# Router of a mixture of experts: the first pair of experts gathered in float32, the high and low halves split later, filler matmuls on TensorE

## Chip, cores and metric

One core of one Trainium2 chip. The metric is the device time of one launch in microseconds (us); the median of three runs of the kernel before is 2560.29 us. Everything is float32 at the interface; weights come from HBM.

## The reference

Two transformer layers (each a mixer, a layer norm, a hierarchical mixture of experts and a layer norm), and behind them a second block of other layers that the change doesn't touch. What matters here is the mixture of experts, once per layer, on 256 tokens of width 1024:

```python
xf = x.reshape(n, d)                                   # 256 x 1024
grp_logits = xf @ w_grp + b_grp                        # 4 groups
g_idx = argmax(grp_logits); p_grp = softmax(grp_logits)[g_idx]
exp_logits = (xf @ w_exp + b_exp).reshape(n, 4, 8)
top_l, top_e = lax.top_k(exp_logits[g_idx], 2)         # two experts of the group
gate = p_grp[:, None] * softmax(top_l)
...
hdn = silu(xb @ w_gate[e]) * (xb @ w_up[e])            # 1024 -> 512
y = hdn @ w_down[e]                                    # 512 -> 1024
out[token] += gate * y
x = layer_norm(ALPHA * x + out)
```

The 32 experts have 6 MB of weights each, and all of them are read in each layer.

## The kernel before, in words

**Stages.** Mixer of layer 0, mixture of experts 0 ("stage 0"), mixer of layer 1, mixture of experts 1 ("stage 1"), then the second block. An expert gets 64 slots; tokens beyond that go through a loop at the end (line 957 on) that the change doesn't touch.

**Weights.** `load_pair` (line 692) issues twelve loads of 1 MB for two experts: four of gate, four of up, four of down. All are issued on SP's queue, in a fixed order, and each waits there until its buffer is free; what stands behind a waiting load waits too. The buffers form a ring of 18 slots (`moe_ring`: the tags W, V, S, X, H and last `c_phase`). The slots belong to tensors of the mixer or the router until these are dead. The last slot, `c_phase`, holds the gain and bias rows of the first layer norm (`rows`, shown as `phase` in the profile), whose last reader is `residual`. Load 19 uses the first slot again.

**The router** (`moe`, line 680 on). `ln_norm` normalises the tokens: ScalarE takes the first 128, VectorE the second. The logits were already multiplied in `Moe.feed` while the mixer ended; `logits` corrects them for mean and deviation. `first_max` finds the group and the two experts on VectorE, a chain of some twenty small dependent operations that ends in `sel` (`m_sel`). In program order behind it stands `hilo` on the normalised tokens, four times: ScalarE casts a piece to fp32r (`xh`), VectorE subtracts (`xl`). Two matmuls with triangular and all-ones matrices (`lt`) turn `sel` into positions `pos`.

**The first gather.** `hots(0)` compares positions with slot numbers and gives one-hot matrices for four experts (`m_P`), and the same scaled by the gates (`m_PG`). `gather` multiplies `xh` and `xl` with the one-hots, 256 slots at once, and ScalarE evacuates with the norm's gain and bias into `xg`. Then `residual` writes ALPHA times the normalised tokens (with gain and bias rows) over the tokens themselves (`r_out = xn`), in four operations on VectorE. The factor `al` is made from an element of the one-hots, so that the scheduler can't put the residual ahead of them.

**The loop over 16 pairs.** `gate_up` (64 matmul instructions in the trace), `hidden`, `down`, and the scatter of the pair before; every second pair gathers the next four experts. TensorE's order in the loop is the program's; elsewhere the tile scheduler orders each engine.

Of the kernel before, what the change touches and what calls it, by code (L numbers as in the profile page):

```python
# [8 lines left out]
F32 = mybir.dt.float32  # L9
F32R = mybir.dt.float32r  # L10
I32 = mybir.dt.int32
U8 = mybir.dt.uint8
AF = mybir.ActivationFunctionType
ALU = mybir.AluOpType
# [3 lines left out]
P = 128  # L18
D = 1024
T = 256  # L20
ALPHA = 4.0 ** 0.25
# [8 lines left out]
NT4 = 2  # L30
NX = 4
NH = 9


C2 = {}
# [90 lines left out]
class K:  # L126
# [33 lines left out]
    def H(self, dt=F32):  # L160
        return self.big.tile([P, NH_F], dt, name=self.nm("H"), tag="H", bufs=NH)

# [150 lines left out]

    def ln_norm(self, out, r, between=None):

        mu, rs = self.ln_stats(r)
        nb = self.tl([P, 2], "ln_nb", 2)
        self.stt(nb, mu, -1.0, rs, ALU.mult, ALU.mult)
        if between is not None:
            between(nb, rs)  # L320
        self.act(out[:, 0], r[:, 0], AF.Identity, scale=rs[:, 0:1], bias=nb[:, 0:1])
        self.ts(out[:, 1], r[:, 1], rs[:, 1:2], ALU.mult, nb[:, 1:2], ALU.add)
        return nb, rs


# [49 lines left out]


def mixer_a(k, x_tm, moe):

    A, nc = k.A, k.nc
# [219 lines left out]
def bc(ap, shape):  # L599
    return ap.to_broadcast(shape)  # L600


class Moe:
# [49 lines left out]
    def feed(self, r, c):  # L653

        k, V = self.k, self.k.nc.vector
        if self.rT is None:
            self.rT = k.H()[:, :2048].rearrange("p (k t) -> p k t", k=8)
            self.lps = [k.pq(), k.pq()]
        for j in range(2 * c, 2 * c + 2):
            ps = k.pq()  # L660
            for m in range(2):
                kk = 2 * j + m
                for i in range(2):
                    k.tr(ps[:, (2 * m + i) * P : (2 * m + i + 1) * P], r[:, i, kk * P : (kk + 1) * P])
            v = ps.rearrange("p (k t) -> p k t", k=2)
            k.acopy(self.rT[:, 2 * j], v[:, 0])
            V.tensor_copy(self.rT[:, 2 * j + 1], v[:, 1])
        for kk in range(4 * c, 4 * c + 4):
            for i in range(2):
                k.mm(self.lps[i][:, 0:36], self.rT[:, kk, i * P : (i + 1) * P], self.wgb[:, 0, kk, :],  # L670
                     start=kk == 0, stop=kk == 7)
# [6 lines left out]
def moe(k, l, r_in, bufs, gb, rows, csb, lps, lt, then):  # L678
    A, nc = k.A, k.nc
    V = nc.vector  # L680
    wg, wu, wd = A["moe_w_gate"][l], A["moe_w_up"][l], A["moe_w_down"][l]
    cst = k.c_m
    iota1 = cst[:, 128:192]
# [3 lines left out]
    def ld(src, kk, n):  # L687
        w = k.wslot()[:, : kk * n].rearrange("p (k f) -> p k f", k=kk)
        k.dma(w, src)
        return w  # L690

    def load_pair(es):

        out = [([], [], []) for _ in es]
        for n, (w, kk, h) in enumerate([(wg, 8, 0), (wg, 8, 1), (wu, 8, 0), (wu, 8, 1), (wd, 4, 0), (wd, 4, 1)]):
            for j, e in enumerate(es):
                v = w[e].rearrange("(p k) f -> p k f", p=P)[:, h * kk // 2 : (h + 1) * kk // 2, :]
                out[j][n // 2].append(ld(v, kk // 2, v.shape[2]))
        return out

    ws0 = load_pair([0, 1])


    xn, xh, xl = (t[:, :2048].rearrange("p (i d) -> p i d", i=2) for t in bufs)
# [34 lines left out]
    sel = k.tl([P, 2, 32], "m_sel", 1, F32R)  # L739
# [2 lines left out]
    k.add(v48(sel), oh1, oh2)  # L742
    k.mul(v48(sel), v48(sel), og)

    perm = lambda t, i, c: t[:, i].rearrange("t (k p) -> t k p", k=8)[:, :, c // 8 : c // 8 + 64]
    for i in range(2):
        for c in range(0, 1024, 512):
            k.hilo(perm(xh, i, c), perm(xl, i, c), xn[:, i, c : c + 512].rearrange("t (p k) -> t k p", k=8))

    pps = k.pq()  # L750
    for j in range(2):
        k.mm(pps[:, 64 * j : 64 * j + 64], lt[:, j], sel.rearrange("p i e -> p (i e)"))
    pos = k.tl([P, 2, 32], "m_pos", 1)
    cnt = k.tl([P, 32], "m_cnt", 1)
    V.tensor_copy(cnt, pps[:, 64:96])
    k.stt(pos[:, 0], pps[:, 0:32], 1.0, sel[:, 0], ALU.add, ALU.mult)
    k.stt(pos[:, 1], pps[:, 32:64], 1.0, cnt, ALU.add, ALU.add)
    k.mul(pos[:, 1], pos[:, 1], sel[:, 1])
    k.add(cnt, cnt, pps[:, 96:128])

    for j in range(2):
        k.mul(m4[:, 2], m4[:, j], ohg)
# [11 lines left out]
    G = k.tl([P, 2, 32], "m_G", 1)  # L774
# [7 lines left out]
    nb = k.tl([P, 32], "m_nb", 1)  # L782
# [6 lines left out]
    for s in (1, 2, 4, 8, 16):  # L789
        a, b = c0[:, cur], c0[:, 1 - cur]  # L790
# [31 lines left out]

    r_out = xn

    def residual(pt):

        al = k.tl([P, 1], "m_al", 1)
        k.ts(al, pt[:, 1, 255:256], 0.0, ALU.mult, ALPHA, ALU.add)
        for i in range(2):
            k.stt(r_out[:, i], xn[:, i], al, rows[:, 0:1024], ALU.mult, ALU.mult)  # L830
            k.stt(r_out[:, i], rows[:, 1024:2048], al, r_out[:, i], ALU.mult, ALU.add)

    def gather(pt, n, out):

        per = 512 // n
        for j in range(0, 8, per):
            ps = k.pq()
            for m in range(per):
                o = ps[:, m * n : (m + 1) * n]
                f = slice((j + m) * P, (j + m + 1) * P)  # L840
                for i in range(2):
                    k.mm(o, xh[:, i, f], pt[:, i], start=i == 0, stop=False)
                    k.mm(o, xl[:, i, f], pt[:, i], start=False, stop=i == 1)
            for m in range(per):
                kk = j + m
                k.act(out[:, kk], ps[:, m * n : (m + 1) * n], AF.Identity, scale=gb[:, 0, kk : kk + 1], bias=gb[:, 1, kk : kk + 1])

    def gate_up(ws, xg, s0):

        gu = []  # L850
        for m in range(2):
            ps = k.pd()
            for kk in range(8):
                for j in range(2):
                    k.mm(ps[64 * j : 64 * j + 64, :], xg[:, kk, s0 + 64 * j : s0 + 64 * j + 64], ws[j][m][kk // 4][:, kk % 4, :],
                         start=kk == 0, stop=kk == 7)
            gu.append(ps)
        return gu
# [40 lines left out]
    def onehots(pos_v, g_v, n):  # L899

        pt = k.tl([P, 2, n * 64], "m_P", 1, F32R)
        pg = k.tl([P, 2, n * 64], "m_PG", 1)
        v = lambda t: t.rearrange("p i (e s) -> p i e s", e=n)
        for i in range(2):
            sh = [P, n, 64]
            io = bc(iota1[:, None, :], sh)
            k.tt(v(pt)[:, i], io, bc(pos_v[:, i, :, None], sh), ALU.is_equal)
            k.mul(v(pg)[:, i], v(pt)[:, i], bc(g_v[:, i, :, None], sh))
        return pt, pg

    def transposed(pg, o):
        ps = k.pq()
        for i in range(2):
            k.tr(ps[:, i * P : (i + 1) * P], pg[:, i, o : o + P])
        return ps[:, :T]

    def slots(pg, o):

        ps = transposed(pg, o)
        oh, gs = k.tl([P, T], "m_pgT", 2, F32R), k.tl([P, 1], "m_gs", 2)  # L920
        k.red(gs, ps, ALU.add)
        k.ts(oh, ps, 0.0, ALU.is_gt)
        return oh, gs

    def hots(q):
        return onehots(pos[:, :, 4 * q : 4 * q + 4], G[:, :, 4 * q : 4 * q + 4], 4)

    def gathered(pt):
        xg = k.H()[:, :2048].rearrange("p (k s) -> p k s", k=8)
        gather(pt, 256, xg)  # L930
        return xg

    pt, pg = hots(0)
    xg = gathered(pt)
    residual(pt)
    prev = None
    with k.tc.manual_schedule(engines={mybir.EngineType.PE}):
        for p in range(16):
            q, o = p // 2, P * (p % 2)
            ws = load_pair([2 * p, 2 * p + 1]) if p else ws0  # L940
            g, u = gate_up(ws, xg, o)
            oh, gs = slots(pg, o)
            if o and q < 7:
                pt, pg = hots(q + 1)
                xg = gathered(pt)
            hT = hidden(g, u)
            if prev is not None:
                scatter(*prev)
            prev = (oh, *down(ws, hT, gs))
        scatter(*prev)  # L950
# [6 lines left out]
    with k.tc.For_i(0, n_ov, 1) as it:  # L957
# [4 lines left out]
        e = nc.sync.value_load(evi[0:1, ds(it, 1)], min_val=0, max_val=31)  # L962
        ws = ([], [], [])
        for n, (w, kk, h) in enumerate([(wg, 8, 0), (wg, 8, 1), (wu, 8, 0), (wu, 8, 1), (wd, 4, 0), (wd, 4, 1)]):
            v = w[ds(e, 1)][0].rearrange("(p k) f -> p k f", p=P)[:, h * kk // 2 : (h + 1) * kk // 2, :]
            ws[n // 2].append(ld(v, kk // 2, v.shape[2]))
        pt, pg = onehots(pc, gc, 1)
        xg = k.H()[:, :512].rearrange("p (k s) -> p k s", k=8)
# [8 lines left out]
        for m in range(2):  # L977
            ps = k.pd()
            for kk in range(8):
                for j in range(2):  # L980
                    k.mm(half(ps, j)[:, :256], xg[:, kk, :], ws[m][kk // 4][:, kk % 4, 256 * j : 256 * j + 256],
                         start=kk == 0, stop=kk == 7)
            gu.append(ps[:, :256])
        g, u = gu
# [17 lines left out]
        for i in range(2):  # L1002
            for j in range(2):
                ps = k.pq()
                k.mm(ps, half(pgT, j)[:, i * P : (i + 1) * P], half(y, j))
                o = r_out[:, i, j * 512 : (j + 1) * 512]
# [870 lines left out]
def body(tc, A, out):  # L1877
    from contextlib import ExitStack

    with ExitStack() as es:  # L1880
# [3 lines left out]
        with tc.tile_pool(name="b1", bufs=1) as b1:  # L1884
            k.big = b1
            dense_ring = w + [("V", NV, b1, 2048)] * NV
            moe_ring = dense_ring + [("S", 1, b1, 2048)] + [("X", NX, b1, 2048)] * NX + [("H", NH, b1, NH_F)] * 4 + [("c_phase", 1, b1, 2048)]
            k.set_ring(dense_ring)
# [103 lines left out]
```

## Time and profile before

| | |
|---|---|
| runs | 2560.29, 2560.14, 2571.59 us; median 2560.29 |
| profiled execution | 2567.35 us, of which the span is 2565.5 us |
| busy share of the span | TensorE 93%, VectorE 54%, ScalarE 41% |
| mean granted TensorE clock | 0.975 |
| mean DMA rate | 251 GB/s |
| stage 0, first gate matmul | 172.69 us |
| stage 1, first gate matmul | 837.98 us |

Times in the trace count from the start of the span. PE is TensorE's matmul, PEld its weight load, DVE VectorE, ACT ScalarE, SP the engine that issues the DMAs. L184 is the helper for matmuls, L187 for transposes, L190 for activations, L193 for copies on ScalarE, L196 for tensor-tensor operations, L213 for the fused scalar-tensor-tensor operations, L181 for DMAs; so tile names tell more than lines. A row of windows gives start and end, length, busy time and count for each engine, granted clock, DMA share and GB/s.

### The profile page before, as it was taken

How to read it: one execution, taken by the hardware profiler on the slowest of the kernel's cores; microseconds unless marked ns; L12 is line 12 of the kernel's file. 1: busy time of each engine (PE TensorE's matmuls, PEld its weight loads, DVE VectorE, ACT ScalarE, POOL GpSimd, SP SyncE). 2: the span in 40 equal slices, each digit the busy share in tenths (PEclk: the TensorE clock that was granted, in tenths of full speed). 3: DMA queues.
4: the chain of work that ended last, by engine and by line, in shares of the span. 5: the costliest groups of instructions: out<-in, count | busy, mean ns of one | idle time of the engine just before them, and what ended most of it. 6: DMA issues, size and time to landing. Idle time of an engine off the chain costs nothing.

```text
span 2565.5 us, 38758 instructions
## 1 busy us (share of the span) xinstructions
PE 2383.6 (93%) x15416; PEld 1748.8 (68%) x15416; DVE 1379.7 (54%) x2844; ACT 1062.1 (41%) x2138; POOL 18.5 (1%) x27
## 2 busy tenths in 40 slices
PE   8979998988787999889979999999998999999999
PEld 7754433334665443333368988899998898889999
DVE  6962222212676322222268878756556887766654
ACT  3421211111532211111147775646454777565654
POOL 0000000000200000000000000000000000000000
PEclk9989999999888999999979999999999999999999
DMA  8569999998535899999945533355553553445553
GB/s 302 168 267 420 421 420 421 420 421 361 183 131 197 366 420 420 421 420 420 400 155 182 173 108 125 107 168 163 179 179 118 186 169 108 134 130 181 181 181 115
DMA packets 189821, 644.14 MB, mean 251 GB/s; under 512 B 21891, under 2 KB 36277, under 8 KB 139589
## 3 DMA queue, kind: packets, MB, share of 16 engines
q1 hardware_dynamic: 189636, 641.63, 66.6%
q8 instruction: 122, 2.00, 0.3%
q14 instruction: 63, 0.51, 0.1%
HBM read 640.46 MB, written 1.12 MB: 250 GB/s over the span
## 4 chain that ended last, share of the span: by engine, by line
PE 53%; DMA 13%; DVE 5%; ACT 3%; issue 1%; ACTq 0%; SPq 0%; DVEq 0%
PE pd L184 44%; PE pq L184 7%; DMA w<-in_moe_w_up 5%; DMA w<-in_moe_w_down 5%; DMA w<-in_moe_w_gate 3%; PE pq L187 2%; DVE Y L196 1%; ACT Y L193 1%; DVE r L213 0%; ACT cb L190 0%; DVE H L196 0%; ACT r L190 0%; DVE cb L209 0%; DVE Xl L196 0%; DVE sg L209 0%
## 5 line engine op out<-in xcount | busy, mean ns | idle before, releaser
L184 PE MATMUL pd<-U,Y 128*128 128x272 f32 (+1 forms) x7792 | 1011.4, 288 | 18.6 <-ACT U L193 12.8
L184 PEld LDWEIGHTS pd<-U,Y 128*128 128x128 f32 x7792 | 979.8, 189 | 35.2 <-ACT U L193 14.2
L196 DVE TENSOR_TENSOR Y<-w,Y 128x1024 fp32r<-128x1024 f32 x344 | 419.6, 1222 | 265.1 <-ACT Y L193 262.4
L184 PE MATMUL pd<-w,H 128*64 128x512 f32 (+1 forms) x2112 | 483.9, 592 | 53.6 <-DMA w<-in_moe_w_up 37.8
L193 ACT CAST Y<-w 128x1024 fp32r<-128x1024 f32 x344 | 359.4, 1047 | 329.8 <-PE pd L184 299.3
L184 PEld LDWEIGHTS pd<-w,H 128*64 128x64 f32 x2112 | 159.1, 138 | 371.7 <-issue 257.1
L184 PE MATMUL pd<-w,m_hT 128*64 128x512 f32 x1040 | 230.4, 595 | 1.8 <-ACT m_hT L193 1.8
L184 PEld LDWEIGHTS pd<-w,m_hT 128*64 128x64 f32 x1040 | 71.6, 137 | 143.0 <-issue 139.0
L213 DVE SCALAR_TENSOR_TENSOR t4k<-pd,m_gs,t4k 128x512 fp32r<-128x512 f32 x64 | 48.1, 751 | 194.4 <-ACT t4k L190 191.9
L196 DVE TENSOR_TENSOR t2k<-t2k,pd 128x512 f32<-128x512 f32 (+1 forms) x33 | 22.4, 679 | 229.0 <-PE pd L184 229.0
L190 ACT ACTIVATE t4k<-pd,m_gs 128x512 fp32r<-128x512 f32 x64 | 44.0, 687 | 235.8 <-PE pd L184 132.1
L213 DVE SCALAR_TENSOR_TENSOR t2k<-t2k,pd 128x512 f32<-128x512 f32 (+1 forms) x33 | 22.4, 680 | 217.8 <-ACT t2k L190 217.8
L190 ACT ACTIVATE H<-pq,m_gb 128x256 f32<-128x256 f32 (+1 forms) x136 | 62.7, 556 | 147.5 <-PE pq L184 147.5
L190 ACT ACTIVATE t2k<-pd 128x512 f32<-128x512 f32 (+1 forms) x37 | 21.9, 591 | 233.4 <-PE pd L184 233.4
L184 PE MATMUL pd<-Xh,H 128*128 128x512 f32 (+1 forms) x320 | 105.6, 402 | 4.3 <-ACT H L193 4.2
L196 DVE TENSOR_TENSOR H<-H,pq 128x512 f32<-128x512 f32 x132 | 82.0, 682 | 26.3 <-PE pq L184 26.3
L193 ACT COPY m_hT<-pq 128x512 f32<-128x512 f32 (+1 forms) x34 | 19.6, 577 | 175.2 <-PE pq L187 170.3
L213 DVE SCALAR_TENSOR_TENSOR r<-pd,cw,r 128x270 f32<-128x270 f32 (+1 forms) x192 | 87.8, 492 | 3.9 <-ACT r L190 2.4
L193 ACT CAST Xh<-w 128x2048 fp32r<-128x2048 f32 (+4 forms) x34 | 57.3, 1689 | 70.4 <-PE pd L184 54.2
L184 PE MATMUL pd<-Z,Y 128*128 128x272 f32 (+1 forms) x512 | 84.2, 286 | 0.0
L196 DVE TENSOR_TENSOR Xl<-w,Xh 128x2048 fp32r<-128x2048 f32 (+4 forms) x34 | 69.0, 2033 | 27.0 <-ACT Xh L193 26.8
L184 PE MATMUL pd<-H,Xh 128*128 128x256 f32 (+1 forms) x352 | 68.7, 296 | 7.0 <-DVE H L196 4.6
(397 smaller groups left out, 2565.6 us busy)
## 6 DMA issues: line engine op xcount, KB each, us to landing
w<-in_moe_w_gate SPq DMA_DIRECT2D x130, 1024.0 KB
w<-in_moe_w_down SPq DMA_DIRECT2D x130, 1024.0 KB
w<-in_moe_w_up SPq DMA_DIRECT2D x130, 1024.0 KB
w<-in_w_in SPq DMA_DIRECT2D x76, 1024.0 KB
w<-in_w_mlp_up SPq DMA_DIRECT2D x32, 1024.0 KB
w<-in_w_mlp_down SPq DMA_DIRECT2D x32, 1024.0 KB
w<-in_w_ssd_down SPq DMA_DIRECT2D x16, 1024.0 KB
w<-in_ev_w_in SPq DMA_DIRECT2D x14, 1024.0 KB
```

The lines of the kernel that those rows point to most:

```text
L184: return self.nc.tensor.matmul(out, l, r, start=start, stop=stop, **kw)
L187: return self.nc.tensor.transpose(out, in_, self.ident[: in_.shape[0], : in_.shape[0]])
L190: return self.nc.scalar.activation(out, in_, func, **kw)
L193: return self.nc.scalar.copy(out, in_)
L196: return self.nc.vector.tensor_tensor(out=out, in0=a, in1=b, op=op)
L213: return self.nc.vector.scalar_tensor_tensor(out=out, in0=a, scalar=s, in1=b, op0=op0, op1=op1)
```

## The change

1. `ln_norm` in the router: both halves of the tokens are normalised by ScalarE. In `feed` the last two transposed banks are copied by ScalarE alone.
2. Twelve filler matmuls (`FILL`), `ones` times a piece of the tokens ahead of the norm, go to a bank that nobody reads.
3. The positions take four smaller matmuls, which add the second half's offset in PSUM; VectorE then makes `pos` in one operation.
4. The first pair is gathered from the normalised tokens themselves: `xn` in float32 against the one-hots of two experts (`hot0(0)`), evacuated half by ScalarE and half by VectorE into `xgs[:, 0]`.
5. The one-hots of experts 2 and 3 and all four `hilo` are held behind the last two evacuations (`issue_after`). The second pair is gathered the old way, in TensorE's program behind the first pair's gate and up, into `xgs[:, 1]`.
6. `residual` takes the constant ALPHA, without the dependency on the one-hots.

```diff
     def ln_norm(self, out, r, between=None):
         self.act(out[:, 0], r[:, 0], AF.Identity, scale=rs[:, 0:1], bias=nb[:, 0:1])
-        self.ts(out[:, 1], r[:, 1], rs[:, 1:2], ALU.mult, nb[:, 1:2], ALU.add)
+        if between is not None:
+            self.act(out[:, 1], r[:, 1], AF.Identity, scale=rs[:, 1:2], bias=nb[:, 1:2])
+        else:
+            self.ts(out[:, 1], r[:, 1], rs[:, 1:2], ALU.mult, nb[:, 1:2], ALU.add)
...
+            if c:
+                k.acopy(self.rT[:, 2 * j : 2 * j + 2], v)
+            else:
+                k.acopy(self.rT[:, 2 * j], v[:, 0])
+                V.tensor_copy(self.rT[:, 2 * j + 1], v[:, 1])
...
+    idle = k.pd()
+    for j in range(FILL):
+        k.mm(idle[:, 0:256], k.ones, r_in[:, 1, 512:768])
...
     pps = k.pq()
-    for j in range(2):
-        k.mm(pps[:, 64 * j : 64 * j + 64], lt[:, j], sel.rearrange("p i e -> p (i e)"))
+    k.mm(pps[:, 0:64], lt[:, 0], sel.rearrange("p i e -> p (i e)"), start=True, stop=False)
+    k.mm(pps[:, 32:64], lt[:, 1], sel[:, 0], start=False, stop=True)
+    for i in range(2):
+        k.mm(pps[:, 64:96], lt[:, 1], sel[:, i], start=i == 0, stop=i == 1)
...
+    hot0(0)
+    xgs = k.H()[:, :2048].rearrange("p (h k s) -> p h k s", h=2, k=8)
+    for j in range(0, 8, 4):
+        ps = k.pq()
+        for m in range(4):
+            o = ps[:, m * P : (m + 1) * P]
+            for i in range(2):
+                k.mm(o, xn[:, i, j + m :: 8], pt0[:, i, 0:128].bitcast(F32), start=i == 0, stop=i == 1)
+        for m in range(4):
+            kk = j + m
+            o, g, b = ps[:, m * P : (m + 1) * P], gb[:, 0, kk : kk + 1], gb[:, 1, kk : kk + 1]
+            if m % 2:
+                ev_d = k.ts(xgs[:, 0, kk], o, g, ALU.mult, b, ALU.add)
+            else:
+                ev_a = k.act(xgs[:, 0, kk], o, AF.Identity, scale=g, bias=b)
...
+    with k.tc.issue_after(ev_a.ins), k.tc.issue_after(ev_d.ins):
+        hot0(2)
+        for i in range(2):
+            for c in range(0, 1024, 512):
+                k.hilo(perm(xh, i, c), perm(xl, i, c), xn[:, i, c : c + 512].rearrange("t (p k) -> t k p", k=8))
...
-    def residual(pt):
-        al = k.tl([P, 1], "m_al", 1)
-        k.ts(al, pt[:, 1, 255:256], 0.0, ALU.mult, ALPHA, ALU.add)
+    def residual():
         for i in range(2):
-            k.stt(r_out[:, i], xn[:, i], al, rows[:, 0:1024], ALU.mult, ALU.mult)
-            k.stt(r_out[:, i], rows[:, 1024:2048], al, r_out[:, i], ALU.mult, ALU.add)
+            k.stt(r_out[:, i], xn[:, i], ALPHA, rows[:, 0:1024], ALU.mult, ALU.mult)
+            k.stt(r_out[:, i], rows[:, 1024:2048], ALPHA, r_out[:, i], ALU.mult, ALU.add)
...
-            g, u = gate_up(ws, xg, o)
+            g, u = gate_up(ws, xg if q else xgs[:, o // P], o if q else 0)
             oh, gs = slots(pg, o)
+            if p == 0:
+                gather(pt[:, :, 128:256], 128, xgs[:, 1])
```

SP's queue in stage 0 before, where the ring comes to its end (w_251 is load 17, w_252 load 18, w_253 load 19; in brackets the engines waited for):

```order
L181 DMA w_250_1657<-in_moe_w_gate 128x2048 [waits DMAHW3_49,DVE_49]
L181 DMA w_251_1659<-in_moe_w_up 128x2048 [waits DMAHW4_49,DVE_49,PE_49]
L181 DMA w_252_1661<-in_moe_w_up 128x2048 [waits DMAHW5_49,DVE_49]
L181 DMA w_253_1663<-in_moe_w_up 128x2048 [waits DMAHW6_49,PE_49]
L181 DMA w_254_1665<-in_moe_w_up 128x2048 [waits DMAHW7_49,PE_49]
```

The same place after:

```order
L182 DMA w_250_1691<-in_moe_w_gate 128x2048 [waits DMAHW3_49,DVE_49]
L182 DMA w_251_1693<-in_moe_w_up 128x2048 [waits DMAHW4_49,PE_49,Activation_49]
L182 DMA w_253_1697<-in_moe_w_up 128x2048 [waits DMAHW5_49,PE_49]
L182 DMA w_252_1695<-in_moe_w_up 128x2048 [waits DMAHW6_49,DVE_49]
L182 DMA w_254_1699<-in_moe_w_up 128x2048 [waits DMAHW7_49,PE_49]
```

Load 19 has moved ahead of load 18; load 18 waits for VectorE in both. VectorE before, around the residual (the four operations with `phase`; `m_cum` is a running sum for the overflow loop):

```order
L196 TENSOR_TENSOR m_oh_205_1408<-m_oh_205_1408,m_sc_1406 128x64
L213 SCALAR_TENSOR_TENSOR m_nb_1470<-m_cnt_1445,m_nb_1470 128x32
L213 SCALAR_TENSOR_TENSOR H_135<-H_135,m_al_1566,phase_1178 128x1024
L196 TENSOR_TENSOR m_G_1465<-m_oh_204_1407,m_oh_205_1408 128x64
L213 SCALAR_TENSOR_TENSOR m_nb_1470<-m_cnt_1445,m_nb_1470 128x32
L213 SCALAR_TENSOR_TENSOR H_135<-phase_1178,m_al_1566,H_135 128x1024
```

VectorE after, ahead of the residual (`H_1454` is `xgs`, `H_1087` is `xl`, `t2k` belongs to the overflow loop's tables):

```order
L211 TENSOR_SCALAR H_1454<-pq_1468,m_gb_1167 128x128
L197 TENSOR_TENSOR m_P_1451<-cm_109,m_pos_1449 128x128 x2
L197 TENSOR_TENSOR H_1087<-H_135,H_1086 128x8x64 x4
L846 CAST m_evi_1538<-m_ev_1534 128x8
L197 TENSOR_TENSOR t2k_1528<-t2k_1528,m_cex_1530 128x224
L197 TENSOR_TENSOR m_PG_1557<-m_P_1451,m_G_1507 128x256
L217 TENSOR_REDUCE m_base_1541<-t2k_1528 128x7
L197 TENSOR_TENSOR m_PG_1557<-m_P_1451,m_G_1507 128x256
L197 TENSOR_TENSOR m_base_1541<-m_base_1541,cm_109 128x7
L197 TENSOR_TENSOR t2k_1528<-t2k_1528,m_pos_1449 128x224
L211 TENSOR_SCALAR m_base_1541<-m_base_1541 128x7
L214 SCALAR_TENSOR_TENSOR H_135<-H_135,phase_1178 128x1024
```

Before, the residual begins a few operations behind the one-hots, and the subtractions into `xl` stood far ahead, between the steps of `first_max`; after, evacuations, one-hots, subtractions, gates and tables stand ahead of it. TensorE after, in the router:

```order
L185 MATMUL pd_1373<-H_1088,ones 128x256 x10
L185 MATMUL pq_1444<-m_sel_1441,m_lt_1196 128x64
L185 MATMUL pq_1444<-m_sel_1441,m_lt_1196 128x32 x3
L185 MATMUL pq_1455<-m_P_1451,H_135 128x128 x8
L185 MATMUL pq_1468<-m_P_1451,H_135 128x128 x8
L185 MATMUL pd_1566<-w_1349,H_1454 64x512
```

Ten of the fillers stand between the logits and the positions; sixteen matmuls of 128 columns replace 32 of 256 ahead of the first gate.

More of the change, by code (lines that the diff above doesn't have):

```diff
@@ L32 @@
 NH = 9
+FILL = 12
 C2 = {}
@@ L665, in feed @@
             v = ps.rearrange("p (k t) -> p k t", k=2)
-            k.acopy(self.rT[:, 2 * j], v[:, 0])
-            V.tensor_copy(self.rT[:, 2 * j + 1], v[:, 1])
+            if c:
[3 more added lines that the diff above has]
+                V.tensor_copy(self.rT[:, 2 * j + 1], v[:, 1])
         for kk in range(4 * c, 4 * c + 4):
@@ L743, in moe @@
     k.mul(v48(sel), v48(sel), og)
-    perm = lambda t, i, c: t[:, i].rearrange("t (k p) -> t k p", k=8)[:, :, c // 8 : c // 8 + 64]
+    pps = k.pq()
+    k.mm(pps[:, 0:64], lt[:, 0], sel.rearrange("p i e -> p (i e)"), start=True, stop=False)
+    k.mm(pps[:, 32:64], lt[:, 1], sel[:, 0], start=False, stop=True)
     for i in range(2):
-        for c in range(0, 1024, 512):
-            k.hilo(perm(xh, i, c), perm(xl, i, c), xn[:, i, c : c + 512].rearrange("t (p k) -> t k p", k=8))
-    pps = k.pq()
@@ L751, in moe, with hot0 @@
-    for j in range(2):
-        k.mm(pps[:, 64 * j : 64 * j + 64], lt[:, j], sel.rearrange("p i e -> p (i e)"))
-    pos = k.tl([P, 2, 32], "m_pos", 1)
+        k.mm(pps[:, 64:96], lt[:, 1], sel[:, i], start=i == 0, stop=i == 1)
+    pos = k.tl([P, 2, 32], "m_pos", 1)
+    k.stt(pos, pps[:, 0:64].rearrange("p (i e) -> p i e", i=2), 1.0, sel, ALU.add, ALU.mult)
+    pt0 = k.tl([P, 2, 256], "m_P", 1, F32R)
+    io2, sh2 = bc(iota1[:, None, :], [P, 2, 64]), [P, 2, 64]
+    def hot0(o):
+        for i in range(2):
+            k.tt(pt0[:, i, 64 * o : 64 * o + 128].rearrange("p (e s) -> p e s", e=2), io2, bc(pos[:, i, o : o + 2, None], sh2),
+                 ALU.is_equal)
@@ L754, in moe @@
     cnt = k.tl([P, 32], "m_cnt", 1)
     V.tensor_copy(cnt, pps[:, 64:96])
[L756 to L759, printed above, removed]
+    perm = lambda t, i, c: t[:, i].rearrange("t (k p) -> t k p", k=8)[:, :, c // 8 : c // 8 + 64]
+    with k.tc.issue_after(ev_a.ins), k.tc.issue_after(ev_d.ins):
[3 more added lines that the diff above has]
+                k.hilo(perm(xh, i, c), perm(xl, i, c), xn[:, i, c : c + 512].rearrange("t (p k) -> t k p", k=8))
@@ L931, in gathered @@
         return xg
-    pt, pg = hots(0)
-    xg = gathered(pt)
-    residual(pt)
+    pt = pt0
+    pg = k.tl([P, 2, 256], "m_PG", 1)
+    for i in range(2):
+        k.mul(pg[:, i].rearrange("p (e s) -> p e s", e=4), pt[:, i].rearrange("p (e s) -> p e s", e=4),
+              bc(G[:, i, 0:4, None], [P, 4, 64]))
+    residual()
     prev = None
```

## Prediction

> **What bounds the kernel now.** I read the slices of the page first, then the chain of waits, then windows of both mixture-of-experts stages. For over a quarter of the span (the 700 us of the two windows below) the DMA engines are full: the weights of 32 experts are streamed twice.
>
> Windows of the two stages (length, busy time of each engine, granted clock, DMA share, GB/s), one piece of the chain that ended last, and the group of the expert loads:
>
> ```profile
> 300.00:600.00 300.00, 273.48 (x1286) 110.92 (x1284) 66.76 (x119) 43.78 (x80) 0.82 (x2) 1.00 1.01 421
> 860.00:1260.00 400.00, 374.55 (x1788) 154.81 (x1784) 95.03 (x168) 62.69 (x114) 0.00 (x0) 1.00 1.01 421
> ...
> 1251.76 19.84 DMA w<-in_moe_w_up
> ...
> w<-in_moe_w_gate SPq DMA_DIRECT2D x130, 1024.0 KB
> ```
>
> DMA share 1.01 at 421 GB/s without a hole, and the chain consists of transfers up to the last load. A load of 1024 KB (1.0486 MB) takes 1.0486/421 = 2.49 us. So a stage lasts (number of loads left) x 2.49 us from the moment at which the queue runs again after its last hole. That hole is in the router:
>
> ```profile
> 168.00:170.00 2.00, 2.00 (x12) 2.00 (x11) 2.00 (x11) 0.21 (x1) 0.00 (x0) 0.50 0.24 90
> 170.00:172.00 2.00, 2.00 (x17) 2.00 (x17) 2.00 (x5) 1.82 (x5) 0.00 (x0) 0.88 0.00 0
> ...
> 174.00:176.00 2.00, 2.00 (x12) 0.72 (x10) 2.00 (x8) 0.00 (x0) 0.00 (x0) 1.00 0.00 0
> 176.00:178.00 2.00, 2.00 (x12) 0.68 (x10) 1.90 (x8) 0.00 (x0) 0.00 (x0) 1.00 0.90 246
> ```
>
> About 8 us without bytes. The issues on SP's queue, its waits, and the last operation of the residual on VectorE, in stage 0 and stage 1, tell what ends it:
>
> ```profile
> 155.88 0.33 SPq L181 DMA_DIRECT2D w<-in_moe_w_up  x1
> 175.04 0.33 SPq L181 DMA_DIRECT2D w<-in_moe_w_up  x1
> 176.37 0.33 SPq L181 DMA_DIRECT2D w<-in_moe_w_up  x1
> 840.07 0.33 SPq L181 DMA_DIRECT2D w<-in_moe_w_up  x1
> ...
> SPq L181 <- DVE m_cum L196: 37.8, 2, 18.9
> ...
> 173.74 1.28 DVE L213 SCALAR_TENSOR_TENSOR H<-phase,m_al,H 128x1024 f32<-128x1024 f32 x1
> 838.77 1.27 DVE L213 SCALAR_TENSOR_TENSOR H<-phase,m_al,H 128x1024 f32<-128x1024 f32 x1
> ```
>
> The ring has 18 slots. Loads 1 to 17 are out at 155.88. Load 18 takes the slot of the gain rows (`phase`), so it waits for their last reader: the residual ends at 173.74 + 1.28 = 175.02 and the load is issued at 175.04; in stage 1, 838.77 + 1.27 = 840.04 and 840.07. The wait is put down to `m_cum`, the small operation beside it, twice 18.9 us. Load 19 needs a slot of the first pair's gate weights, free only at 176.37. **So the stage is paced by two things that end together: the residual on VectorE and the first half of the first gate matmuls on TensorE.**
>
> **The change, part by part.** All times below are stage 0 on the clock of the trace of before. The path to the selection on VectorE:
>
> ```profile
> 153.57 0.21 DVE L310 BATCH_NORM_AGGREGATE ln_mv<-ln_st 128x2 f32<-128x12 f32 x1
> 153.85 0.76 DVE L667 COPY H<-pq 128x256 f32<-128x256 f32 x2
> 154.52 0.16 DVE L209 TENSOR_SCALAR lnr_h<-ln_mv 128x2 f32<-128x2 f32 x1
> ...
> 157.38 0.80 DVE L210 TENSOR_SCALAR H<-H,lnr_y,ln_nb 128x1024 f32<-128x1024 f32 x1
> 158.10 0.21 DVE L216 TENSOR_REDUCE m_m<-m_L 128x8 f32<-128x64 f32 x1
> 158.34 0.23 DVE L196 TENSOR_TENSOR m_t<-m_L,m_m 128x64 f32<-128x64 f32 x1
> ...
> 163.72 0.21 DVE L213 SCALAR_TENSOR_TENSOR m_ing<-m_oh,m_L 128x64 f32<-128x64 f32 x1
> ...
> 164.22 0.22 DVE L196 TENSOR_TENSOR m_t<-m_ing,m_m 128x64 f32<-128x64 f32 x1
> 164.48 0.23 DVE L196 TENSOR_TENSOR m_t<-m_t,cm 128x64 f32<-128x64 f32 x1
> 165.51 0.23 DVE L196 TENSOR_TENSOR m_sel<-m_sel,m_ohg 128x64 fp32r<-128x64 f32 x1
> ```
>
> The two copies go to ScalarE: the root starts 0.04 us behind the aggregate (153.82), not at 154.52, 0.70 gained. The normalisation of the second half leaves VectorE: 158.10 - 157.38 = 0.72, less 0.12 of latency, 0.60 gained. The four low-half subtractions leave this path: 158.34 to 163.72 is 5.38 us for four dependent steps, which cost 164.48 - 164.22 = 0.26 each where nothing stands between them, and 0.3 for small operations between: 1.34, so 4.04 gained. The selection is ready at 165.74 - 5.34 = 160.4.
>
> TensorE next: the logits, the gather before, the same gather for a later pair, the first gate and up, and a float32 product over `ones`:
>
> ```profile
> 153.87 1.99 PE L184 MATMUL pq<-t4k,H 128*128 128x36 f32 x16
> 167.50 5.27 PE L184 MATMUL pq<-m_P,H 128*128 128x256 f32 x32 [1.01 <-DVE m_pos L196]
> 172.69 13.95 PE L184 MATMUL pd<-w,H 128*64 128x512 f32 x64
> 209.83 3.90 PE L184 MATMUL pq<-m_P,H 128*128 128x256 f32 x32
> 799.11 2.26 PE L184 MATMUL pq<-t4k,ones 128*128 128x288 f32 x4 [4.38 <-DVE t4k L196]
> ...
> L184 PEld LDWEIGHTS pq<-m_P,H 128*128 128x128 f32 x32 | 5.1, 250 | 1.1 <-ACT m_sc L190 1.1
> ```
>
> A float32 matmul shows as two instructions (8 logits calls, x16). The fillers are 24 instructions; the last 20 follow the logits at about 155.7 and cost between 0.21 (half of a 512-column instruction pair's 13.95/32 = 0.436) and 0.26 (2.26/4 at half the clock, 256 of 288 columns) each, so they end between 159.9 and 160.8, about when the selection is ready: they cost nothing to half a microsecond, and I take nothing. From the selection to the first gather matmul it was 167.50 - 165.74 = 1.76; two small VectorE steps fewer and TensorE at full clock make it about 1.25: 161.65. The gather is again 32 instructions, now half as wide and float32; the trace has none of this form. Its ends are the logits' 1.99/16 = 0.12 (full clock, also 128 weight columns) and 0.25 (the weight load above, mostly at half clock): 3.9 or 8 us. I take 0.12, because TensorE comes to it busy. TensorE reaches the first gate at 165.55, not 172.69, and load 19's slot is free 3.5 us later (a quarter of 13.95), at 169.0.
>
> **That is half of the pacing pair. The other half goes the other way.** The residual overwrites the normalised tokens, so it stays behind everything that reads them: in the new order behind the eight evacuations, the second one-hots, the four casts and subtractions and the gates:
>
> ```profile
> L196 DVE TENSOR_TENSOR H<-H,H 128x512 fp32r<-128x512 f32 x4 | 4.3, 1064 | 0.5 <-ACT H L193 0.5
> L193 ACT CAST H<-H 128x512 fp32r<-128x512 f32 x4 | 4.2, 1114 | 0.0
> L190 ACT ACTIVATE H<-pq,m_gb 128x256 f32<-128x256 f32 x8 | 3.9, 561 | 3.3 <-PE pq L184 3.3
> ...
> 168.52 1.28 DVE L213 SCALAR_TENSOR_TENSOR H<-H,m_al,phase 128x1024 f32<-128x1024 f32 x1
> 169.72 0.22 DVE L196 TENSOR_TENSOR m_G<-m_oh,m_oh 128x64 f32<-128x64 f32 x1
> 173.23 0.42 DVE L196 TENSOR_TENSOR m_PG<-m_P,m_G 128x256 f32<-128x256 f32 x1
> 173.56 0.17 DVE L791 COPY m_cum<-m_cum 128x4 f32<-128x4 f32 x1
> ```
>
> - Gather done 165.55. The second bank's evacuations alternate: ScalarE about 0.45 (0.56 at twice the width), VectorE about 0.27 (0.38 at twice), ScalarE 0.45, with the hand-overs: 166.9.
> - ScalarE then makes its four casts, 1.04 each (4.2 in all); the fourth subtraction (1.06) follows the fourth cast: 172.2.
> - Five operations of 0.33 (173.56 - 173.23: a 256-wide one holds the engine so long) and some small ones: 174.15.
> - The residual: four of 1.20 (169.72 - 168.52), with three 0.31 reductions and products between: 5.9, ending at **180.05**, which is 5.0 later than 175.02.
>
> Load 18 waits for that, and now load 19 stands ahead of it on SP's queue: it uses the hole (issued 169.0), which is worth 2.49. Behind load 18 everything else waits, but by then a whole gate and up have freed their slots and the loads go out in one burst; in stage 1 the old restart was thin, worth 0.4. Sum: + 5.0 - 2.49 - 0.2 = +2.3 a stage, **+4.6 us in all**. The profiled execution took 2567.35 (span 2565.5, 1.85 around it); it would take 2572.0. The runs' median was 2560.29, so I predict **2565 us**. TensorE's 7 us head start and the second half's gather (another 3.9 behind the first pair's up) change nothing: TensorE is the faster of the two, and after a few pairs it waits for loads again.
>
> **The clock.** The granted clock in two neighbouring windows:
>
> ```profile
> 156.40:156.80 0.40, 0.00 (x0) 0.00 (x0) 0.33 (x3) 0.06 (x1) 0.00 (x0) 1.00 1.02 430
> 156.80:157.20 0.40, 0.00 (x0) 0.00 (x0) 0.40 (x3) 0.40 (x1) 0.00 (x0) 0.51 1.01 430
> ```
>
> The last matmul ended at 155.86, and the clock was halved at 156.8, 0.95 us later. So a short pause such as that between 160.9 and 161.65 could still lose the clock in the middle of the gather; half of the gather at 0.25 instead of 0.12 is 16 x 0.13 = 2.1 us more a stage, 2569 in all. The Trainium skill (TensorE: Matmul & The Clock Gate, Part 1) says that the clock falls only after an idle window of about 3.4 us. By that rule the fillers hold it through the gather and the sum stays 2565; this trace, with 0.95 us, does not bear the rule out as worded.
>
> **The rivals.** *Load 18 doesn't hold the queue* (or TensorE paces the stage): then the queue runs again with load 19. The old restart, reckoned back from 178.0 by 2 us at 246 GB/s, was 178.0 - 1.17 = 176.83, 1.8 behind the issue at 175.04; the new one would be 169.0 + 1.8 = 170.8: -6.0 a stage, 2548, about at the bound of 0.5%. For it: TensorE is 7 us earlier. Against: 175.04 and 840.07 match the residual to 0.03 us, and load 18 waits for VectorE in the new order too. Chance 0.08. *The gather runs cold and slow*: 0.25 us an instruction, 8 us; evacuations, casts, residual and load 18 all move 4.1 later, +6.4 a stage, 2573. It is slower by over 0.5% from about 8 us of gather on. For it: 0.95 us was enough to lose the clock; against: five microseconds of fillers. Chance 0.12. *The fillers miss their aim* is the 2569 above, inside the forecast's range. The forecast: 0.80.
>
> **How the numbers follow.** 0.5% (12.8 us) is about what a measurement of this kernel can tell from no change. The first rival lies at that bound on the one side (0.06 of its 0.08 beyond it), the second on the other (0.09 of its 0.12): faster 0.06, slower 0.09, within 0.85. The residual's end is uncertain by about 1 us down and 4 up, a stage: 2563 to 2573; the runs of before lie between 2560 and 2572. Range 2556 to 2574.
>
> **What would show it.** In the changed profile: the selection some 5 us earlier; fillers up to its end; the first gate near 165.5; one load at 169, then a DMA hole of 8 to 9 us ending about 1.5 us behind the residual, at 180; DMA without a hole from there. It is wrong if load 18 is issued before the residual's last operation, or if the hole ends before 177.

## The result, and the profile after

The changed kernel takes 2577.56 us (median of 9 runs, 2575.62 to 2582.0) where the kernel before took 2561.3 us beside it: a ratio of 1.0054, 95% interval 1.0044 to 1.0065. (The ratio is estimated from all runs of both; the quotient of the two medians is 1.0063.) In a second sitting the ratio was 1.0049 (1.0030 to 1.0067). It is slower by half a per cent; forecast were 2565 us and a range up to 2574.

**Where the time went.** The last normalisation aggregate on VectorE (start us, duration) marks the start of stage 0, its end (the aggregate of the layer norm behind it), the start of stage 1 and its end. The last three of the four in the trace of before, then all four of after:

```profile
656.12 0.21 DVE L310 BATCH_NORM_AGGREGATE ln_mv<-ln_st 128x2 f32<-128x12 f32 x1
818.67 0.21 DVE L310 BATCH_NORM_AGGREGATE ln_mv<-ln_st 128x2 f32<-128x12 f32 x1
1295.28 0.21 DVE L310 BATCH_NORM_AGGREGATE ln_mv<-ln_st 128x2 f32<-128x12 f32 x1
```

```profile
153.15 0.21 DVE L311 BATCH_NORM_AGGREGATE ln_mv<-ln_st 128x2 f32<-128x12 f32 x1
662.45 0.21 DVE L311 BATCH_NORM_AGGREGATE ln_mv<-ln_st 128x2 f32<-128x12 f32 x1
824.88 0.21 DVE L311 BATCH_NORM_AGGREGATE ln_mv<-ln_st 128x2 f32<-128x12 f32 x1
1307.69 0.21 DVE L311 BATCH_NORM_AGGREGATE ln_mv<-ln_st 128x2 f32<-128x12 f32 x1
```

Before, from 153.57: stage 0 lasts 502.55 us, the piece between the stages 162.55, stage 1 476.61. After: 509.30, 162.43, 482.81. So +6.75 and +6.20, 12.95 us together, and nothing between them. These are single executions: in another one of the changed kernel the stages last 506.25 and 482.51, so +3.70 and +5.90, 9.60 together. One stage of one execution is thus good to some 3 us, and only the direction and the rough size can be read from it. The clock of after stands 0.42 us ahead of that of before (153.15 against 153.57); that much is to be added to its times when they are set against the forecast's.

**TensorE in the router of stage 0** (timeline of after: start, busy us, what): fillers, positions, first gather, first gate and up. Then the gather of stage 1, and windows with the granted clock (third figure from the end) for both:

```profile
155.90 4.56 PE L185 MATMUL pd<-H,ones 128*128 128x256 f32 x20
160.11 0.70 PE L185 MATMUL pq<-m_sel,m_lt 128*128 128x64 f32 x4
161.55 7.87 PE L185 MATMUL pq<-m_P,H 128*128 128x128 f32 x32 [0.73 <-DVE m_P L197]
169.35 13.96 PE L185 MATMUL pd<-w,H 128*64 128x512 f32 x64
...
833.29 7.88 PE L185 MATMUL pq<-m_P,H 128*128 128x128 f32 x32 [0.74 <-DVE m_P L197]
...
160.00:168.00 8.00, 7.27 (x34) 7.15 (x33) 5.39 (x36) 1.12 (x3) 0.00 (x0) 1.00 0.99 414
836.00:838.00 2.00, 2.00 (x11) 2.00 (x9) 0.01 (x1) 0.46 (x1) 0.00 (x0) 0.50 0.99 414
```

The fillers end with the selection and hold the clock at 1.00, as meant. But the gather takes 7.87 us, 0.246 an instruction, twice the forecast, and in stage 1, where the clock fell to 0.50 in its midst, it takes 7.88: the same. So the clock is not what makes this gather slow.

**VectorE** (timeline of after): the selection, an evacuation, the subtractions, and the first and last operation of the residual; below, that last operation of stage 1:

```profile
159.52 0.22 DVE L197 TENSOR_TENSOR m_sel<-m_sel,m_ohg 128x64 fp32r<-128x64 f32 x1
171.00 0.40 DVE L211 TENSOR_SCALAR H<-pq,m_gb 128x128 f32<-128x128 f32 x1
171.90 4.20 DVE L197 TENSOR_TENSOR H<-H,H 128x512 fp32r<-128x512 f32 x4
177.80 1.22 DVE L214 SCALAR_TENSOR_TENSOR H<-H,phase 128x1024 f32<-128x1024 f32 x1
182.17 1.22 DVE L214 SCALAR_TENSOR_TENSOR H<-phase,H 128x1024 f32<-128x1024 f32 x1
...
853.91 1.21 DVE L214 SCALAR_TENSOR_TENSOR H<-phase,H 128x1024 f32<-128x1024 f32 x1
```

**SP's queue** (issues) and the DMA windows (last two columns: share, GB/s):

```profile
173.03 0.33 SPq L182 DMA_DIRECT2D w<-in_moe_w_up  x1
183.42 0.81 SPq L182 DMA_DIRECT2D w<-in_moe_w_up  x2
...
855.15 0.33 SPq L182 DMA_DIRECT2D w<-in_moe_w_up  x1
...
170.00:174.00 4.00, 4.00 (x21) 1.29 (x18) 3.86 (x9) 3.60 (x5) 0.00 (x0) 1.00 0.03 6
174.00:176.00 2.00, 2.00 (x12) 0.72 (x10) 2.00 (x3) 0.98 (x1) 0.00 (x0) 1.00 0.87 270
176.00:178.00 2.00, 2.00 (x14) 0.59 (x10) 2.00 (x10) 0.60 (x1) 0.00 (x0) 1.00 0.57 242
178.00:184.00 6.00, 6.00 (x33) 2.33 (x30) 6.00 (x10) 0.00 (x0) 0.00 (x0) 1.00 0.00 0
184.00:186.00 2.00, 2.00 (x20) 2.00 (x20) 1.93 (x6) 0.55 (x2) 0.00 (x0) 1.00 0.77 205
200.00:600.00 400.00, 371.43 (x1764) 153.35 (x1762) 93.50 (x166) 61.68 (x112) 0.82 (x2) 1.00 1.01 421
```

The chain stands as forecast: residual ends at 182.17 + 1.22 = 183.39, load 18 goes out at 183.42 (in stage 1 855.12 and 855.15); one load, number 19, is carried in the hole (270 + 242 GB/s over 2 us each is 1.02 MB); then nothing until 186 - 2 x 205/421 = 185.03, and from there no hole. Only all of it is later than forecast.

### The profile page after: what moved, and what is told of

Read it like the earlier page. It is cut to its first block, busy times and chain, and to the rows that moved or that the text cites. A ratio compares the mean times of both kernels' runs of the same rounds, so it can differ in the third digit from the quotient of the medians.

```text
span 2578.0 us, 39001 instructions
## 1 busy us (share of the span) xinstructions
PE 2412.7 (94%) x15532; PEld 1773.8 (69%) x15532; DVE 1379.7 (54%) x2842; ACT 1067.3 (41%) x2148; POOL 18.5 (1%) x27
## 4 chain that ended last, share of the span: by engine, by line
PE 50%; DMA 16%; DVE 4%; ACT 3%; issue 1%; ACTq 0%; SPq 0%; DVEq 0%
PE pd L185 42%; PE pq L185 7%; DMA w<-in_moe_w_up 5%; DMA w<-in_moe_w_down 5%; DMA w<-in_moe_w_gate 5%; PE pq L188 1%; ACT Y L194 1%; DVE Y L197 1%; DVE r L214 0%; ACT cb L191 0%; ACT r L191 0%; DVE H L197 0%; DVE Xl L197 0%; DMA csd<-cr 0%; DVE cb L210 0%
## 5 line engine op out<-in xcount | busy, mean ns | idle before, releaser
L185 PE MATMUL pd<-U,Y 128*128 128x272 f32 (+1 forms) x7792 | 1012.3, 288 | 17.3 <-ACT U L194 12.8
L191 ACT ACTIVATE H<-pq,m_gb 128x256 f32<-128x256 f32 (+2 forms) x144 | 65.6, 535 | 179.9 <-PE pq L185 167.3
L185 PE MATMUL pq<-m_P,H 128*128 128x256 f32 (+2 forms) x608 | 86.2, 301 | 3.5 <-DVE m_P L197 3.5
L185 PEld LDWEIGHTS pq<-m_P,H 128*128 128x128 f32 x608 | 82.9, 212 | 4.1 <-DVE m_P L197 2.5
```

The costliest lines, as they stand in the source:

```text
L185: return self.nc.tensor.matmul(out, l, r, start=start, stop=stop, **kw)
L191: return self.nc.scalar.activation(out, in_, func, **kw)
```

## The experiments

What is to be told apart: (a) does the residual's hold on one slot set the stage, or does TensorE; (b) why does a gather instruction cost 0.246 us. Ratios are to the kernel before in the same sitting; after had 1.0054.

**The slot not lent.**

```diff
-            moe_ring = dense_ring + [("S", 1, b1, 2048)] + [("X", NX, b1, 2048)] * NX + [("H", NH, b1, NH_F)] * 4 + [("c_phase", 1, b1, 2048)]
+            moe_ring = dense_ring + [("S", 1, b1, 2048)] + [("X", NX, b1, 2048)] * NX + [("H", NH, b1, NH_F)] * 4
```

> The changed kernel with 17 slots in the ring of expert weights: the gain rows' slot is no longer lent to a load, so no load waits for the residual. Residual theory (the stage streams again when the residual's last operation frees that slot): load 18 now takes a slot of the first pair's gate weights and is issued near 173 instead of 184.3 us of stage 0, the DMA hole ends near 175 instead of 185, with one load of 2.49 us more still to come: -7.7 us a stage, about 2562 us. TensorE theory (the late gate and the gathers set the stage, the slot is beside the point): the residual's wait is not missed, one load less lies ahead, 2577 to 2582 us.

Measured 2564.23 us, ratio 0.9999 (0.9989 to 1.0008). Its issue and windows of stage 0 (its times run 0.78 us later than those of after):

```profile
173.83 0.33 SPq L182 DMA_DIRECT2D w<-in_moe_w_up  x1
...
172.00:174.00 2.00, 2.00 (x12) 0.64 (x10) 1.89 (x5) 2.00 (x3) 0.00 (x0) 1.00 0.00 0
174.00:176.00 2.00, 2.00 (x12) 0.72 (x10) 2.00 (x3) 1.80 (x2) 0.00 (x0) 1.00 0.58 131
176.00:178.00 2.00, 2.00 (x12) 0.65 (x10) 2.00 (x6) 0.60 (x1) 0.00 (x0) 1.00 0.98 414
```

With gather, gate and residual where they were, the stage starts again near 175.4 instead of 185, and the whole loss is gone, although the ring is one slot shorter. So in the changed kernel it is the residual that sets the restart, not TensorE. With the residual's hold gone TensorE is next: the load at 173.83 goes out 3.68 us behind the first gate matmul (170.15), as load 19 did in the changed kernel (169.35 and 173.03).

**The residual early, into another tile.**

```diff
-    hot0(0)
+    hot = hot0(0)
+    r_out = r_in
+    with k.tc.issue_after(hot.ins):
+        for i in range(2):
+            k.stt(r_out[:, i], xn[:, i], ALPHA, rows[:, 0:1024], ALU.mult, ALU.mult)
+            k.stt(r_out[:, i], rows[:, 1024:2048], ALPHA, r_out[:, i], ALU.mult, ALU.add)
...
-    residual()
```

(The count and the tables are put behind the evacuations, so that they don't fill VectorE ahead of them.)

> The changed kernel with the residual written to another tile (the router's input, dead by then), so that it need not wait for the readers of the normalised tokens; it runs on VectorE right behind the first one-hots, while TensorE gathers, and the tables stand behind the casts and subtractions. Residual theory: the residual ends near 167, load 18 goes out then, load 19 with the gate's first quarter near 173, the hole ends near 174.8 instead of 185 with as many loads left: -10 us a stage, about 2557 us. TensorE theory: gather, gate and up lie where they lay, so 2577 us.

Measured 2558.1 us, ratio 0.9977 (0.9964 to 0.9991): 0.77% below after, expected were 0.8. Gather, residual, the issue of load 18 and the clock inside the gather:

```profile
162.17 7.88 PE L185 MATMUL pq<-m_P,H 128*128 128x128 f32 x32 [0.73 <-DVE m_P L197]
...
164.41 2.35 DVE L214 SCALAR_TENSOR_TENSOR H<-phase,H 128x1024 f32<-128x1024 f32 x2
...
166.79 0.33 SPq L182 DMA_DIRECT2D w<-in_moe_w_up  x1
...
164.00:166.00 2.00, 2.00 (x10) 2.00 (x10) 2.00 (x3) 0.00 (x0) 0.00 (x0) 0.50 1.01 422
172.00:174.00 2.00, 2.00 (x12) 0.68 (x10) 1.80 (x4) 2.00 (x3) 0.00 (x0) 1.00 0.17 70
```

The residual ends at 166.76, load 18 follows at 166.79. The nearly empty part of the hole is down to some 2 us around 173, where load 19 waits for the gate, with thinner windows on both sides of it.

**Adjacent stationary blocks.** The stationary block is the operand of `k.mm` that the weight loads of the trace (PEld) bring to TensorE, here 128 features of the tokens. With this edit the first pair's features come out in another order than its weights want.

```diff
-                k.mm(o, xn[:, i, j + m :: 8], pt0[:, i, 0:128].bitcast(F32), start=i == 0, stop=i == 1)
+                k.mm(o, xn[:, i, (j + m) * P : (j + m + 1) * P], pt0[:, i, 0:128].bitcast(F32), start=i == 0, stop=i == 1)
```

> The changed kernel with the 16 stationary blocks of the float32 gather taken as 128 adjacent features instead of every eighth one; the features of the first pair come out in another order than the weights want, nothing else changes. Stride theory (the 0.24 us of a gather instruction is the price of loading a stationary block with elements 32 bytes apart): 0.12 us each, gather 3.9 us instead of 7.9, gate, residual and load 18 all 3.9 earlier, -7.8 us in all, about 2570 us. Float32 theory (any float32 block costs that): gather 7.9 us, 2577 us.

Measured 2571.45 us, ratio 1.0029 (1.0016 to 1.0042). The gather:

```profile
162.64 3.81 PE L185 MATMUL pq<-m_P,H 128*128 128x128 f32 x32 [0.73 <-DVE m_P L197]
...
179.19 1.22 DVE L214 SCALAR_TENSOR_TENSOR H<-phase,H 128x1024 f32<-128x1024 f32 x1
...
819.65 0.21 DVE L311 BATCH_NORM_AGGREGATE ln_mv<-ln_st 128x2 f32<-128x12 f32 x1
1298.12 0.21 DVE L311 BATCH_NORM_AGGREGATE ln_mv<-ln_st 128x2 f32<-128x12 f32 x1
```

0.119 us an instruction, the value of the forecast. The time falls by 0.25% of 2577.56, 6.4 us, where 7.8 were expected. The rows agree: this run's times are 1.09 us later than those of after, so the residual's end at 180.41 is 4.07 earlier, which is what the gather saves; stage 1 lasts 478.47 us, 4.34 and 4.04 less than in the two executions of after. Float32 is not what costs; the distance between the elements is.

**How far apart.** The same line with `j + m : j + m + 2 * P : 2`, and with 4 for 2 (again other features; one execution each).

> The changed kernel with the stationary blocks of the float32 gather taken as every second feature (elements 8 bytes apart) instead of every eighth (32 bytes); the first pair gets other features, nothing else changes. Read from the profile. If a line of 16 bytes with at least two elements on it costs nothing extra: 0.12 us an instruction, gather 3.8 us. If any gap costs: more than 0.12, up to 0.24 us, gather up to 7.9 us.

> As the run before with every fourth feature (16 bytes). If each element on a line of its own is what costs: 0.24 us an instruction, gather 7.9 us, as with every eighth. If the price grows with the distance: between 0.12 and 0.24 us, gather about 5 to 6 us.

The gathers, of the first and of the second:

```profile
160.63 4.04 PE L185 MATMUL pq<-m_P,H 128*128 128x128 f32 x32 [0.73 <-DVE m_P L197]
```

```profile
160.02 7.70 PE L185 MATMUL pq<-m_P,H 128*128 128x128 f32 x32 [0.74 <-DVE m_P L197]
```

Elements 4, 8, 16 and 32 bytes apart: 3.81, 4.04, 7.70 and 7.87 us. It is a step between 8 and 16 bytes, no slope.

**Without fillers** (`FILL = 0`).

> The changed kernel without the 12 filler products. Clock theory: the granted clock falls to about a half before the selection is ready and the gather begins at that clock, which comes back some 3 us later; gather about 9.5 to 10 us instead of 7.9, residual that much later, +1.6 to 2.1 a stage, about 2581 us. If the fillers do nothing for this gather: 7.9 us, 2577 us; if they are in the way of the selection: below 2575 us.

```profile
161.06 7.90 PE L185 MATMUL pq<-m_P,H 128*128 128x128 f32 x32 [0.73 <-DVE m_P L197]
...
160.00:164.00 4.00, 3.27 (x14) 3.19 (x15) 3.50 (x27) 0.07 (x1) 0.00 (x0) 0.50 1.01 426
```

My expectation failed: with the clock at 0.50 for the first 4.6 us (0.59 is the mean from 164 to 166) the gather takes 7.90 us, as at full clock. Measured 2570.58 us, ratio 1.0028 (1.0014 to 1.0042), which looked like a gain of some 7 us. So after was run once more, beside the next three:

> The changed kernel itself once more, beside the three that follow and the same runs of before: is the gain of some 7 us that the run without fillers showed real? If the fillers cost time, this stays at a ratio of 1.0054 to before, about 2577 us. If it was a difference between two sittings: ratio 1.003, as without fillers.

2577.16 us, 1.0049 (1.0030 to 1.0067). The two intervals overlap, and between the same aggregates the stages are equally long: without fillers 506.35 us (the rows of stage 0 below) and 482.80, in this run of after 506.25 and 482.51:

```profile
152.60 0.21 DVE L311 BATCH_NORM_AGGREGATE ln_mv<-ln_st 128x2 f32<-128x12 f32 x1
658.95 0.21 DVE L311 BATCH_NORM_AGGREGATE ln_mv<-ln_st 128x2 f32<-128x12 f32 x1
```

```profile
152.56 0.21 DVE L311 BATCH_NORM_AGGREGATE ln_mv<-ln_st 128x2 f32<-128x12 f32 x1
658.81 0.21 DVE L311 BATCH_NORM_AGGREGATE ln_mv<-ln_st 128x2 f32<-128x12 f32 x1
```

The fillers change nothing in the stages. What is short in this profiled execution is the piece behind the last of the four aggregates, which the change doesn't touch: 1264.42 us, where all other runs have 1268.69 to 1271.38. Two of those (below) have no fillers either, with 1269.80 and 1270.21, so the fillers aren't seen to be the cause, and what made it short is open. A difference of 0.25% between totals doesn't tell by itself where it comes from. The same with the early residual and no fillers:

> As the run with the early residual alone (gather of every eighth feature), without the fillers. The gather took 7.9 us at half the clock and at full clock, so with the residual out of the way the fillers should be worth nothing: 2558 us, ratio 0.998. If the fillers as such cost time (some 3 us a stage): about 2551 us.

2558.19 us, 0.9975 (0.9962 to 0.9988): no difference to 0.9977. Behind a gather of this kind no gain and no cost of the fillers can be seen.

**Both mends.** The residual as above; the normalised tokens written by ScalarE in the permuted order, so that the stationary blocks, the casts and the subtractions read adjacent elements (the residual's first operation on each half of the tokens now reads the permuted order instead); all eight evacuations on ScalarE.

```diff
+            q = lambda i: r[:, i].rearrange("t (p k) -> t k p", k=8)
+            o = lambda i: out[:, i].rearrange("t (k p) -> t k p", k=8)
+            self.act(o(0), q(0), AF.Identity, scale=rs[:, 0:1], bias=nb[:, 0:1])
...
+                k.mm(o, xn[:, i, (j + m) * P : (j + m + 1) * P], pt0[:, i, 0:128].bitcast(F32), start=i == 0, stop=i == 1)
+            ev_a = ev_d = k.act(xgs[:, 0, kk], o, AF.Identity, scale=g, bias=b)
```

> Both mends at once, and the whole computation: the normalised tokens are written in the permuted order (so every stationary block of the float32 gather is 128 adjacent elements), the residual goes to the other tile behind the first one-hots, the first half's evacuations are all on ScalarE, the tables behind them. Residual and stride theory together: gather 3.8 us, load 19 near 169.4 instead of 173, residual out of the way near 167, hole ended near 171.2 instead of 174.8: -3.5 us a stage against the residual alone, about 2551 us. TensorE theory: gate 4 us earlier than in the changed kernel, 2570 us. If the permuted writing of ScalarE (two operations, perhaps 2.3 us each instead of 1.23) is late for the gather, up to 2 us a stage of this is lost: 2555 us.

Measured 2553.36 us, ratio 0.9954 (0.9935 to 0.9972): faster than both kernels. ScalarE's normalisation and casts, the gather, and the windows where after had its hole:

```profile
154.86 4.39 ACT L191 ACTIVATE H<-H,ln_nb,lnr_y 128x1024 f32<-128x1024 f32 x2 [1.53 <-DVE ln_nb L214]
166.01 2.18 ACT L194 CAST H<-H 128x512 fp32r<-128x512 f32 x4
...
160.78 3.81 PE L185 MATMUL pq<-m_P,H 128*128 128x128 f32 x32 [0.73 <-DVE m_P L197]
...
166.00:168.00 2.00, 2.00 (x12) 0.58 (x9) 1.90 (x8) 2.00 (x5) 0.00 (x0) 1.00 0.83 299
168.00:170.00 2.00, 2.00 (x12) 0.72 (x10) 2.00 (x5) 0.39 (x3) 0.00 (x0) 1.00 0.85 291
```

The hole is nearly closed: 291 GB/s is the least of any window in stage 0. The permuted normalisation takes 4.39 us for the two (2.37 before it was permuted), and still ends at 159.25, ahead of the gather. The two residual operations that read the permuted tokens take 1.96 us each where those of the early residual alone took 1.22; the residual still ends at 166.86, and load 18 goes out at 166.88.

> As the run with both mends, without the fillers. Clock theory for adjacent blocks: the gather starts at half the clock, 0.25 us an instruction until the clock returns some 4 us later, then 0.12: about 6 us instead of 3.8, +2 a stage, 2555 us where the run with fillers has 2551. If the load of a block costs the same at any clock: 3.8 us, 2551 us.

```profile
160.75 5.88 PE L185 MATMUL pq<-m_P,H 128*128 128x128 f32 x32 [0.74 <-DVE m_P L197]
160.00:164.00 4.00, 3.26 (x16) 3.29 (x16) 3.95 (x6) 0.00 (x0) 0.00 (x0) 0.50 1.02 428
164.00:166.00 2.00, 2.00 (x15) 2.00 (x14) 2.00 (x3) 1.47 (x4) 0.00 (x0) 0.73 1.02 406
```

With adjacent blocks the clock does count, as expected: the first 4.3 us at 0.50 (0.73 from 164 to 166 puts its return at about 165.1), and 5.88 us in all instead of 3.81. The total is 2554.04 us, 0.9953 (0.9937 to 0.9969). Twice 2 us would be 0.16%, about half the width of these intervals, so the totals can't say what the 2 us are worth. They do reach the queue: load 19 goes out at 170.24 instead of 168.20. But in the four windows from 166 to 174 the queue moves 283, 303, 246 and 393 GB/s where it moved 299, 291, 360 and 377; by that estimate 0.2 MB, or 0.5 us at 421 GB/s, is lost in stage 0.

## Why the prediction was wrong, point by point

| step, stage 0, clock of before | forecast | measured (after + 0.42) |
|---|---|---|
| selection ready | 160.4 | 160.16 |
| gather starts | 161.65 | 161.97 |
| gather takes | **3.9** | **7.87** |
| first gate starts | 165.55 | 169.77 |
| last evacuation ends | 166.9 | 171.82 |
| last subtraction ends | 172.2 | 176.52 |
| residual ends, load 18 out | 180.05 | 183.81 |
| longer by, per stage | 2.3 | 6.75 and 6.20 (the other execution: 3.70 and 5.90) |

- **What bounds the stage** was right: the queue waits for the residual's hold on the slot, not for TensorE. The run without that slot and the one with the early residual show it; the rival that load 18 doesn't hold the queue is refuted.
- **The selection path** came out within 0.3 us, the fillers ended where they should, and the rest between gather and residual took no longer than forecast (from the end of the gather to the end of the residual 14.0 us, forecast 14.5).
- **The step that failed is "I take 0.12, because TensorE comes to it busy".** The trace of before gave 0.12 and 0.25 for an instruction, and I put the difference down to the clock alone. The logits' 0.12 came from stationary blocks of adjacent elements; the new gather takes every eighth, and that took 0.246 with the clock at 1.00 throughout and at 0.50 for over half of it alike. The row that was nearest in form was not the nearest in access. The residual ended 3.76 us later than forecast, which is the gather's excess (3.97) less a little. Twice 3.8 on top of the 4.6 gives 12.2; the stages grew by 12.95 in one execution and by 9.60 in the other.
- **The 0.25 at the other end was luck.** It is the mean duration of one weight load, and the loads overlap: in the prediction's row 32 of them kept the loader busy for 5.1 us, 0.16 each. With adjacent blocks the mean duration was 0.19 us where an instruction cost 0.119. That 0.25 met the measured 0.246 says nothing for how it was read.
- **The second rival** had the size (0.25 an instruction, 8 us, +12.8 us) and the wrong cause. Its condition, a cold TensorE, did not hold in stage 0 and was not needed; so its chance of 0.12 was that of losing the clock, and the price of the new access at full clock was not asked for. 12.8 us is 0.50% and lies in the measured interval; 2573 lies below the measured 2577.56 in part because it was counted from 2560.29, the median of three runs; the kernel before had medians of 2561.3 beside the result and of 2566.19 and 2564.41 in the later sittings.
- The Trainium skill (Advanced Engine Details and Errata, SBUF Cachelines) states 16-byte lines, and that a read needs at least two hits on a line to run at full speed. The step between 8 and 16 bytes agrees with it. It gives no size of the penalty. The forecast did not weigh it; it would have spoken against the price of adjacent elements.

## What to carry to other kernels

When an operand's access changes, look up a price with the same distance between its elements, and not only the same shape and type: a bound of the estimate is tied to a cause, and another cause can reach it too. Before moving work away from a path, ask which transfer waits for the last reader of a lent buffer: here a dead tile for the result let 4.6 us of VectorE run under the gather and was worth 0.77%, against 0.25% for making the gather itself twice as fast. What an engine gains that doesn't set the stage is seen in its rows and not in the time: TensorE reached the first gate 2.9 us earlier than before (169.77 against 172.69), and the kernel was slower.

## What the runs showed of the hardware

- A matmul instruction of the float32 gather, with the load of its stationary block of 128 columns, took 0.119 us with the block's elements 4 bytes apart, 0.126 at 8, 0.241 at 16 and 0.246 at 32 (3.81, 4.04, 7.70, 7.87 us for 32, at a clock of 1.00). With the clock at 0.50 from the start, the adjacent blocks took 5.88 us (clock back after 4.3 us), the spread ones 7.90 (after 4.6), as at full clock.
- ScalarE reading float32 elements 32 bytes apart took about twice as long: four casts of 512 elements 4.23 us in after, 2.18 with adjacent ones; two normalisations of 1024 elements 2.37 us adjacent in after, 4.39 permuted (the run with both mends). The rows of after:

```profile
155.63 2.37 ACT L191 ACTIVATE H<-H,ln_nb,lnr_y 128x1024 f32<-128x1024 f32 x2 [1.53 <-DVE ln_nb L214]
170.75 4.23 ACT L194 CAST H<-H 128x512 fp32r<-128x512 f32 x4
```

- The clock fell in the midst of the gather, with TensorE busy all the time: 0.50 at 836 to 838 in stage 1 of after, and at 164 to 166 with the early residual; in stage 0 of after it stayed at 1.00. The Trainium skill (TensorE: Matmul & The Clock Gate, Part 1) has it fall after an idle window of about 3.4 us; the longest pause near is the 0.74 us ahead of the gather, so these traces do not agree, and what sets it off here is open.
